# Sharing the products of a group between ScalarE and VectorE in a token-times-weights kernel

## The chip, the cores and the metric

The kernel runs on one core of a Trainium2 chip. The metric is the device time of one execution in microseconds (us). The core has a vector engine (VectorE, DVE in the profile), a scalar engine (ScalarE, ACT), a matrix engine (TensorE, PE), GpSimd (POOL) and a sync engine (SyncE, SP). ScalarE and SyncE issue transfers too; their queues are called ACTq and SPq, and 16 DMA engines carry out what both queues issue.

## What is computed

For each of 16 x 1024 tokens the row of 512 numbers is multiplied by each of the token's two weights, so every row of x gives two rows of the output. The expert indices are not used.

```python
batch, seq, hidden, n_experts, k = 16, 1024, 512, 8, 2
x_expanded = x[:, :, np.newaxis, :].repeat(k, axis=2)
weights = expert_weights[..., np.newaxis]
return (x_expanded * weights).astype(np.float32)
```

That reads 33.6 MB of x and writes 67.1 MB, all float32.

## The kernel before

The 16,384 tokens are cut into 8 groups of 2,048: 128 partitions with T = 16 tokens in each. A group lives in one slot of 64 KB per partition (16 tokens x 2 products x 512 numbers x 4 bytes), and there are three slots. The load of a group (`load`, L120, issued on ScalarE's queue, 4 MB) puts its x into the upper half of the slot; the products then fill the slot from below, in place. In units of 512 numbers, token t's x lies at position 16 + t and its products go to 2t and 2t + 1. So token t may be computed only when the tokens whose x lies at 2t and 2t + 1, tokens 2t - 16 and 2t - 15, have been read.

`ranges(16)` cuts the first 15 tokens into pieces that keep this rule: (0,8), (8,12), (12,14), (14,15). For each piece `products` issues one tensor_tensor on VectorE (L136), which broadcasts x over the two products and the weights over the 512 numbers: 8192, 4096, 2048 and 1024 numbers per partition. Token 15 is left to `last` (L151 to L157), two ACTIVATEs of 512 numbers on ScalarE (L153); the first of them overwrites token 14's x, the second token 15's own x.

The order of the work is written out by hand (manual schedule), so each engine executes its instructions in program order, and a tracker inserts the waits between engines where the tiles' regions meet. First the weights are loaded and spread over the partitions by TensorE transposes (L66 to L102), and the loads of groups 0, 1 and 2 are issued. Then, for each group i: the four products, the two ACTIVATEs, the store of the whole slot on SyncE's queue (L178, 8 MB), and, from group 1 on, the load of group i + 2, which goes into the slot of group i - 1 and so waits on ScalarE's queue until the store of group i - 1 has landed. In the first and the last group the store is in halves: the first 8 tokens right after the first product (L174), the rest at the end (L178).

Of the kernel before, what the change touches and what calls it, by code (L numbers as in the profile page):

```python
# [1 line left out]

# [4 lines left out]


@with_exitstack
def kernel(  # L10
    ctx: ExitStack,
    tc: tile.TileContext,
    x: bass.AP,
    expert_indices: bass.AP,
    expert_weights: bass.AP,
    out: bass.AP,
):
    nc = tc.nc

    batch, seq, hidden = x.shape  # L20
    k = expert_weights.shape[-1]
    P = nc.NUM_PARTITIONS
    ntok = batch * seq
    assert ntok % P == 0

    f32 = mybir.dt.float32
    row = k * hidden


    groups = [16] * 8  # L30
    assert sum(groups) * P == ntok
    TX = max(groups)

    xf = x.rearrange("b s h -> (b s) h")
    of = out.rearrange("b s k h -> (b s) (k h)")
    wf = expert_weights.rearrange("b s k -> (b s) k")

    w_pool = ctx.enter_context(tc.tile_pool(name="w_pool", bufs=1))
    slots = ctx.enter_context(tc.tile_pool(name="slots", bufs=3))
    raw_pool = ctx.enter_context(tc.tile_pool(name="raw_pool", bufs=1))  # L40
    psum = ctx.enter_context(
        tc.tile_pool(name="psum", bufs=2, space=bass.MemoryType.PSUM)
    )

    w_tile = w_pool.tile([P, sum(groups) * k], f32)

    def rows(flat, done, T):
        return flat[done * P : (done + T) * P, :].rearrange("(p a) n -> p (a n)", a=T)

    B = 8
    M = P // B
    ident = w_pool.tile([P, P], f32)
    nc.gpsimd.memset(ident, 0.0)  # L55
    nc.gpsimd.affine_select(  # L56
        out=ident,
        in_=ident,
        compare_op=mybir.AluOpType.not_equal,
        fill=1.0,  # L60
        base=0,
        pattern=[[-1, P]],
        channel_multiplier=1,
    )

    def weights_in(head, G, T):  # L66
        raw_tile = raw_pool.tile([G * M, B * T * k], f32, name=f"raw{T}_tile")
        nc.sync.dma_start(
            out=raw_tile,
            in_=wf[head * P : (head + G * T) * P, :].rearrange(  # L70
                "(q a) n -> q (a n)", a=B * T
            ),
        )
        return raw_tile

    def weights_spread(raw_tile, head, G, T):
        n = T * k
        col_tile = raw_pool.tile([n, G * P], f32, name=f"col{T}_tile")
        cols = col_tile.rearrange("c (q r) -> c q r", r=B)
        step = 4  # L80
        for r0 in range(0, B, step):
            up_tile = psum.tile([n, step, G * M], f32)
            for r in range(step):
                nc.tensor.transpose(  # L84
                    up_tile[:, r, :],
                    raw_tile[:, (r0 + r) * n : (r0 + r + 1) * n],
                    ident[: G * M, : G * M],
                )
            nc.vector.tensor_copy(  # L89
                out=cols[:, :, r0 : r0 + step],  # L90
                in_=up_tile.rearrange("c r q -> c q r"),
            )
        down_tile = psum.tile([P, G * n], f32)
        for g in range(G):
            nc.tensor.transpose(  # L95
                down_tile[:, g * n : (g + 1) * n],
                col_tile[:, g * P : (g + 1) * P],
                ident[:n, :n],
            )
        nc.vector.tensor_copy(  # L100
            out=w_tile[:, head * k : (head + G * T) * k], in_=down_tile
        )  # L102

    ctx.enter_context(tc.manual_schedule())

    starts = [sum(groups[:i]) for i in range(len(groups))]
    loaded = []

    def load(i):
        if i >= len(groups):
            return
        T = groups[i]
        slot_tile = slots.tile([P, TX * row], f32)
        loaded.append(slot_tile)
        src = rows(xf, starts[i], T)
        at = T * (row - hidden)
        nc.scalar.dma_start(out=slot_tile[:, at : at + T * hidden], in_=src)  # L120


    def ranges(T):
        lo, out = 0, []
        while lo < T - 1:
            hi = lo + 1
            while (hi + 1) * k <= T * (k - 1) + lo and hi < T - 1:
                hi += 1
            out.append((lo, hi))
            lo = hi  # L130
        return out

    def products(slot_tile, T, lo, hi, w_at):
        m = hi - lo
        at = T * (row - hidden) + lo * hidden
        nc.vector.tensor_tensor(  # L136
            out=slot_tile[:, lo * row : hi * row].rearrange(
                "p (t k h) -> p t k h", t=m, k=k
            ),
            in0=slot_tile[:, at : at + m * hidden]  # L140
            .rearrange("p (t h) -> p t h", t=m)
            .unsqueeze(2)
            .to_broadcast([P, m, k, hidden]),
            in1=w_tile[:, w_at + lo * k : w_at + hi * k]
            .rearrange("p (t k) -> p t k", t=m)
            .unsqueeze(3)
            .to_broadcast([P, m, k, hidden]),
            op=mybir.AluOpType.mult,
        )

    def last(slot_tile, T, w_at):  # L151
        for c in range(T * k - k, T * k):
            nc.scalar.mul(  # L153
                out=slot_tile[:, c * hidden : (c + 1) * hidden],
                in_=slot_tile[:, T * row - hidden : T * row],
                mul=w_tile[:, w_at + c : w_at + c + 1],
            )  # L157

    raw_tile = weights_in(0, 8, 16)
    load(0)  # L160
    load(1)
    load(2)
    weights_spread(raw_tile, 0, 8, 16)

    for i, T in enumerate(groups):
        slot_tile = loaded[i]
        outr = rows(of, starts[i], T)
        w_at = starts[i] * k
        done = 0
        for lo, hi in ranges(T):  # L170
            products(slot_tile, T, lo, hi, w_at)
            if i in (0, len(groups) - 1) and done == 0:
                done = hi
                nc.sync.dma_start(  # L174
                    out=outr[:, : done * row], in_=slot_tile[:, : done * row]
                )
        last(slot_tile, T, w_at)
        nc.sync.dma_start(  # L178
            out=outr[:, done * row :], in_=slot_tile[:, done * row : T * row]
        )  # L180
        if i:
            load(i + 2)

# [1 line left out]
_INS = ['x', 'expert_indices', 'expert_weights']  # L185
_OUTS = [((16, 1024, 2, 512), 'float32')]


# [23 lines left out]
```

## Time and profile before

| what | value |
|---|---|
| median of three runs (lowest to highest) | 248.65 us (239.22 to 249.16) |
| the profiled execution's own time | 239.3 us |
| its span, from the first to the last instruction | 237.5 us |
| moved between HBM and the core over the span | 100.80 MB, 424 GB/s |
| VectorE busy | 134.7 us (57%) |
| ScalarE busy | 12.8 us (5%) |
| TensorE busy | 2.9 us (1%) |
| a load, from issue to landing (median) | 32.6 us |
| a whole store, from issue to landing (median) | 35.9 us |

All views below come from one execution, taken by the hardware profiler. Rows of groups of instructions read: line, engine, operation, output <- inputs, shapes, count | busy time in us, mean duration of one in ns | idle time of the engine just before them and what ended most of it. Rows of the timeline read: start in us, length in us, engine, line, operation; in brackets the idle time before, with its releaser. Consecutive instructions of a kind are merged into one row, which then names the shape of the first. Rows of the table by stage read: from:to in us, its length, then the busy time of PE, PEld, DVE, ACT and POOL with the instructions begun or running, the granted clock of TensorE, the share of the DMA engines that was busy, and GB/s. Bytes are counted where a packet's record ends or begins, so single stages can read over 1.00.

### The profile page before, as it was taken

The page shows a single profiled execution, that of the slowest core. Times are in us where ns is not written, and L with a number is a line of the kernel's source. Part 1 is how long each engine was busy: PE and PEld are TensorE (multiplying, and loading weights), DVE is VectorE, ACT ScalarE, POOL GpSimd, SP SyncE. Part 2 cuts the span into 40 slices and gives each one's busy share as a digit, 9 for nine tenths or more (in the row PEclk, how much of TensorE's full clock was granted, in tenths as well). Part 3 has the DMA queues.
Part 4 walks back from the last instruction along what each step waited for, and adds up shares of the span by engine and source line. Part 5 has one row for each costly group of instructions (what it writes and reads, how often), then busy time and mean ns, then how long its engine had stood idle before and what let it go on. Part 6 is the DMA issues. An engine that isn't in the chain of part 4 may idle for free.

```text
span 237.5 us, 184 instructions
## 1 busy us (share of the span) xinstructions
PE 2.9 (1%) x16; PEld 1.9 (1%) x16; DVE 134.7 (57%) x35; ACT 12.8 (5%) x17; POOL 0.7 (0%) x6
## 2 busy tenths in 40 slices
PE   0400000000000000000000000000000000000000
PEld 0300000000000000000000000000000000000000
DVE  0289999999600089900998009970199602995000
ACT  0020020110200000020001100020000200002000
POOL 1000000000000000000000000000000000000000
DMA  7999999999899899899799898998998989989996
GB/s 284 444 441 441 353 441 441 436 447 441 375 419 530 353 441 530 353 441 530 337 458 430 370 524 353 441 530 353 441 530 348 447 386 453 486 353 441 441 441 265
DMA packets 2736, 100.80 MB, mean 424 GB/s; under 512 B 304, under 2 KB 432, under 8 KB 432
## 3 DMA queue, kind: packets, MB, share of 16 engines
q1 hardware_dynamic: 1584, 67.24, 65.5%
q10 hardware_dynamic: 1152, 33.55, 33.2%
HBM read 33.69 MB, written 67.11 MB: 424 GB/s over the span
## 4 chain that ended last, share of the span: by engine, by line
DMA 61%; DVE 28%; ACT 2%; issue 0%; DVEq 0%; ACTq 0%
DMA slot_tile<-in_x_dram 33%; DMA out_dram<-slot_tile 29%; DVE slot_tile L136 28%; ACT slot_tile L153 2%; DVEq L136 0%; ACTq L120 0%
## 5 line engine op out<-in xcount | busy, mean ns | idle before, releaser
L136 DVE TENSOR_TENSOR slot_tile<-slot_tile,w_tile 128x8192 f32<-128x8192 f32 (+3 forms) x32 | 132.9, 4158 | 71.6 <-DMA slot_tile<-in_x_dram 70.7
L153 ACT ACTIVATE slot_tile<-slot_tile,w_tile 128x512 f32<-128x512 f32 x16 | 11.5, 721 | 192.5 <-DVE slot_tile L136 192.3
L89 DVE COPY col_tile<-up_tile 32x512 f32<-32x512 f32 x2 | 1.4, 678 | 9.6 <-PE up_tile L84 9.6
L153 ACT ACT_TABLE_LOAD x1 | 1.3, 1283 | 13.2 <-DMA slot_tile<-in_x_dram 13.2
L84 PE MATMUL up_tile<-ident,raw_tile 128*32 128x128 f32 x8 | 1.9, 411 | 8.4 <-DMA raw_tile<-in_expert_weights_dram 8.4
L84 PEld LDWEIGHTS up_tile<-ident,raw_tile 128*32 128x32 f32 x8 | 1.0, 135 | 8.8 <-issue 8.4
L100 DVE COPY w_tile<-down_tile 128x256 f32<-128x256 f32 x1 | 0.4, 424 | 1.1 <-PE down_tile L95 1.1
L95 PE MATMUL down_tile<-ident,col_tile 32*128 32x32 f32 x8 | 1.1, 292 | 0.8 <-DVE col_tile L89 0.8
L95 PEld LDWEIGHTS down_tile<-ident,col_tile 32*128 32x128 f32 x8 | 0.9, 214 | 1.3 <-DVE col_tile L89 1.3
L56 POOL TENSOR_SCALAR_AFFINE_SELECT ident<-ident 128x128 f32<-128x128 f32 x1 | 0.3, 292 | 0.1
L55 POOL MEMSET ident<- 128x128 f32 x1 | 0.2, 204 | 0.3 <-POOLq L196 0.3
L196 POOL MEMSET const-bfloat16-1.0<- 128x1 bf16 x1 | 0.1, 101 | 0.0
L196 POOL MEMSET const-uint8-127<- 128x1 uint8 x1 | 0.1, 101 | 0.0
L196 POOL MEMSET const-float32-0.0<- 128x1 f32 x1 | 0.1, 98 | 0.2 <-issue 0.2
L196 POOL MEMSET const-float32-1.0<- 128x1 f32 x1 | 0.1, 98 | 0.0
## 6 DMA issues: line engine op xcount, KB each, us to landing
slot_tile<-in_x_dram ACTq DMA_DIRECT2D x8, 4096.0 KB, 32.6
out_dram<-slot_tile SPq DMA_DIRECT2D x4, 4096.0 KB, 19.5
raw_tile<-in_expert_weights_dram SPq DMA_DIRECT2D x1, 128.0 KB, 7.5
out_dram<-slot_tile SPq DMA_DIRECT2D x6, 35.9
```

What stands on the lines that cost most here:

```text
L55: nc.gpsimd.memset(ident, 0.0)
L56: nc.gpsimd.affine_select(out=ident, in_=ident, compare_op=mybir.AluOpType.not_equal, fill=1.0, base=0, pattern=[[-1, P]], channel_multipl ...
L84: nc.tensor.transpose(up_tile[:, r, :], raw_tile[:, (r0 + r) * n : (r0 + r + 1) * n], ident[: G * M, : G * M],)
L89: nc.vector.tensor_copy(out=cols[:, :, r0 : r0 + step], in_=up_tile.rearrange("c r q -> c q r"),)
L95: nc.tensor.transpose(down_tile[:, g * n : (g + 1) * n], col_tile[:, g * P : (g + 1) * P], ident[:n, :n],)
L100: nc.vector.tensor_copy(out=w_tile[:, head * k : (head + G * T) * k], in_=down_tile)
L136: nc.vector.tensor_tensor(out=slot_tile[:, lo * row : hi * row].rearrange("p (t k h) -> p t k h", t=m, k=k), in0=slot_tile[:, at : at + m ...
L153: nc.scalar.mul(out=slot_tile[:, c * hidden : (c + 1) * hidden], in_=slot_tile[:, T * row - hidden : T * row], mul=w_tile[:, w_at + c : w_ ...
L196: nc = _bacc.Bacc("TRN2", target_bir_lowering=False, num_devices=1)
```

## The change

`ranges` and `last` go. A new function `scaled` computes one token by two instructions, one for each weight: two ACTIVATEs on ScalarE or two tensor_scalars on VectorE. ScalarE now makes tokens 6 and 7 in the first half of a group and token 11 in the second; VectorE makes tokens 0 to 5, 8 to 10, 12 and 13, and 14 by tensor_tensors as before, and token 15 by two tensor_scalars at the end. The store of a half in the first and last group comes after the first 8 tokens, as before, and `load` stays as it is.

```diff
-    def ranges(T):
-        lo, out = 0, []
-        while lo < T - 1:
-            hi = lo + 1
-            while (hi + 1) * k <= T * (k - 1) + lo and hi < T - 1:
-                hi += 1
-            out.append((lo, hi))
-            lo = hi
-        return out
...
-    def last(slot_tile, T, w_at):
-        for c in range(T * k - k, T * k):
-            nc.scalar.mul(
-                out=slot_tile[:, c * hidden : (c + 1) * hidden],
-                in_=slot_tile[:, T * row - hidden : T * row],
-                mul=w_tile[:, w_at + c : w_at + c + 1],
-            )
+    def scaled(eng, slot_tile, T, t, w_at):
+        at = T * (row - hidden) + t * hidden
+        for c in range(t * k, t * k + k):
+            out = slot_tile[:, c * hidden : (c + 1) * hidden]
+            x_in = slot_tile[:, at : at + hidden]
+            w = w_tile[:, w_at + c : w_at + c + 1]
+            if eng is nc.scalar:
+                eng.mul(out=out, in_=x_in, mul=w)
+            else:
+                eng.tensor_scalar(
+                    out=out, in0=x_in, scalar1=w, scalar2=None, op0=mybir.AluOpType.mult
+                )
+
+    def first_half(slot_tile, T, w_at):
+        products(slot_tile, T, 0, 6, w_at)
+        scaled(nc.scalar, slot_tile, T, 6, w_at)
+        scaled(nc.scalar, slot_tile, T, 7, w_at)
+
+    def second_half(slot_tile, T, w_at):
+        scaled(nc.scalar, slot_tile, T, 11, w_at)
+        products(slot_tile, T, 8, 11, w_at)
+        products(slot_tile, T, 12, 14, w_at)
+        products(slot_tile, T, 14, 15, w_at)
+        scaled(nc.vector, slot_tile, T, 15, w_at)
...
-        for lo, hi in ranges(T):
-            products(slot_tile, T, lo, hi, w_at)
-            if i in (0, len(groups) - 1) and done == 0:
-                done = hi
-                nc.sync.dma_start(
-                    out=outr[:, : done * row], in_=slot_tile[:, : done * row]
-                )
-        last(slot_tile, T, w_at)
+        first_half(slot_tile, T, w_at)
+        if i in (0, len(groups) - 1):
+            done = T // 2
+            nc.sync.dma_start(
+                out=outr[:, : done * row], in_=slot_tile[:, : done * row]
+            )
+        second_half(slot_tile, T, w_at)
         nc.sync.dma_start(
             out=outr[:, done * row :], in_=slot_tile[:, done * row : T * row]
         )
```

## The prediction

> **What bounds the kernel now.** I first read the page's slices, queues and chain, to see which resource is full. The digits are tenths of a slice's time, the queue rows give packets, bytes and the share of the time of all 16 DMA engines.
>
> ```profile
> span 237.5 us, 184 instructions
> ...
> DVE  0289999999600089900998009970199602995000
> ...
> DMA  7999999999899899899799898998998989989996
> ...
> q1 hardware_dynamic: 1584, 67.24, 65.5%
> q10 hardware_dynamic: 1152, 33.55, 33.2%
> ...
> DMA 61%; DVE 28%; ACT 2%; issue 0%; DVEq 0%; ACTq 0%
> ```
>
> The stores' queue (q1) and the loads' queue (q10) together take 65.5 + 33.2 = 98.7% of the engines' time. So at most 1.3% of 237.5 us, 3.1 us, is left in which the transfers could be packed more tightly. VectorE shows empty slices from the middle on. The chain gives VectorE 28%, but a chain follows one releaser at each step; that the transfers behind that releaser were standing in a queue is not in it. So the next view is transfers by stage. Its last two columns are the busy share of the DMA engines and GB/s.
>
> ```profile
> 2.00:24.00 22.00, 2.92 (x16) 1.93 (x16) 12.54 (x5) 1.28 (x1) 0.00 (x0) 1.00 1.02 430
> 24.00:36.00 12.00, 0.00 (x0) 0.00 (x0) 11.93 (x4) 1.44 (x2) 0.00 (x0) 1.00 0.97 393
> 36.00:60.00 24.00, 0.00 (x0) 0.00 (x0) 23.83 (x7) 1.44 (x2) 0.00 (x0) 1.00 1.01 437
> 60.00:114.00 54.00, 0.00 (x0) 0.00 (x0) 20.60 (x7) 2.88 (x4) 0.00 (x0) 1.00 1.01 437
> 114.00:168.00 54.00, 0.00 (x0) 0.00 (x0) 32.51 (x8) 2.89 (x4) 0.00 (x0) 1.00 0.99 428
> 168.00:200.00 32.00, 0.00 (x0) 0.00 (x0) 16.64 (x4) 1.44 (x2) 0.00 (x0) 1.00 1.06 457
> 200.00:218.00 18.00, 0.00 (x0) 0.00 (x0) 16.64 (x4) 0.92 (x2) 0.00 (x0) 1.00 0.94 408
> 218.00:236.00 18.00, 0.00 (x0) 0.00 (x0) 0.00 (x0) 0.53 (x1) 0.00 (x0) 1.00 0.94 408
> ```
>
> The DMA share is 0.94 or more in every stage, whether VectorE is busy for 23.83 of 24 us (36 to 60) or for none of 18 (218 to 236). The rate has a plateau of 437 GB/s, and computing less would not raise it. The third view, the timeline, shows how much room stands between the arithmetic and the transfers.
>
> ```profile
> 101.05 1.48 ACT L153 ACTIVATE slot_tile<-slot_tile,w_tile 128x512 f32<-128x512 f32 x2 [36.31 <-DVE slot_tile L136]
> 109.53 0.33 ACTq L120 DMA_DIRECT2D slot_tile<-in_x_dram  x1
> 113.24 16.74 DVE L136 TENSOR_TENSOR slot_tile<-slot_tile,w_tile 128x8192 f32<-128x8192 f32 x4 [12.22 <-DMA slot_tile<-in_x_dram]
> 130.01 1.47 ACT L153 ACTIVATE slot_tile<-slot_tile,w_tile 128x512 f32<-128x512 f32 x2 [27.48 <-DVE slot_tile L136]
> 131.51 29.37 SPq L178 DMA_DIRECT2D out_dram<-slot_tile  x2
> 138.49 0.33 ACTq L120 DMA_DIRECT2D slot_tile<-in_x_dram  x1
> 142.27 16.74 DVE L136 TENSOR_TENSOR slot_tile<-slot_tile,w_tile 128x8192 f32<-128x8192 f32 x4 [12.29 <-DMA slot_tile<-in_x_dram]
> ```
>
> A load (L120) goes into the slot that a store has just left, so its issue marks that store's landing. Group 3 is computed at 101.05 + 1.48 = 102.53 and its store can be queued, but the store of group 2 lands only at 109.53: the new store stands 7.0 us in line. Group 4 repeats it: queued at 131.51, the store ahead landing at 138.49, again 7.0 us. Meanwhile VectorE waits 12.3 us per group for a load.
>
> **The change part by part.** The durations of one group are these:
>
> ```profile
> L136 DVE TENSOR_TENSOR slot_tile<-slot_tile,w_tile 128x8192 f32<-128x8192 f32 x8 | 69.5, 8691 | 70.7 <-DMA slot_tile<-in_x_dram 70.7
> L136 DVE TENSOR_TENSOR slot_tile<-slot_tile,w_tile 128x4096 f32<-128x4096 f32 x8 | 35.4, 4425 | 0.3
> L136 DVE TENSOR_TENSOR slot_tile<-slot_tile,w_tile 128x2048 f32<-128x2048 f32 x8 | 18.3, 2292 | 0.3
> L153 ACT ACTIVATE slot_tile<-slot_tile,w_tile 128x512 f32<-128x512 f32 x16 | 11.5, 721 | 192.5 <-DVE slot_tile L136 192.3
> L136 DVE TENSOR_TENSOR slot_tile<-slot_tile,w_tile 128x1024 f32<-128x1024 f32 x8 | 9.8, 1225 | 0.3
> ...
> L89 DVE COPY col_tile<-up_tile 32x512 f32<-32x512 f32 x2 | 1.4, 678 | 9.6 <-PE up_tile L84 9.6
> ```
>
> *Before*, one after the other: 8.69 + 4.43 + 2.29 + 1.23 + 2 x 0.72 = 18.1 us; with the gaps it is 131.51 - 113.24 = 18.27 us from the first product to the store's issue. One token of VectorE's products costs (8691 - 4425) / 4 = 1066 ns, with 4425 - 4 x 1066 = 161 ns for each instruction.
>
> *VectorE's products after*: six tokens 161 + 6 x 1066 = 6.56 us, three tokens 3.36, two 2.29, one 1.23: 13.44 us.
>
> *The two tensor_scalars of token 15*: no row shows this form. The nearest is the 512-element copy, 0.68 us, though it reads PSUM and covers 32 partitions; the line of the products gives 161 + 533 = 0.69. The other end is the fixed 0.16 us alone. I take 0.69, 1.39 for both; the low end is 0.32. The Trainium skill, "VectorE: DVE Perf Modes", the perf-mode tier table, has fp32 tensor_scalar from SBUF at twice the rate of tensor_tensor; worked out from its 1227 ns for 2048 elements and its 0.96 GHz, an estimate for 512 is 0.43 us, and a group would be 0.5 us shorter than my sum. No run here shows it yet.
>
> *Sum of a group after*: 13.44 + 1.39 + 0.1 of gaps = 14.9 us (13.9 to 15.0 between the ends), 3.3 us less than 18.27. The first half is ready after 6.56 instead of 8.69 us, 2.1 us earlier.
>
> *ScalarE*: six ACTIVATEs instead of two, 6 x 0.72 = 4.3 us, beside the products. Tokens 6 and 7 end after 2.9 us, under VectorE's 6.56; token 11 after 4.4 us, when VectorE reaches tokens 12 and 13, which overwrite token 11's input, after 6.56 + 3.36 = 9.9 us. The cover is 5.5 us. Without it the four first ACTIVATEs would add 2.9 us and token 11 another 1.4. In group 0 the 1.28 us that ScalarE is busy between 2 and 24 (its table load) come first, inside the same cover.
>
> *The wait that moves*: ScalarE's queue also issues the loads, and the load of group i+2 waits there until the store of group i-1 has landed. Before, that stood ahead of two late ACTIVATEs; now six early ones of group i+1 are behind it. In the steady part the wait is over at 109.53 and the next slot's data come at 113.24, 138.49 and 142.27 likewise: 3.7 us to spare. Group 2 is the exception:
>
> ```profile
> 13.21 50.03 DVE L136 TENSOR_TENSOR slot_tile<-slot_tile,w_tile 128x8192 f32<-128x8192 f32 x12 [0.66 <-DMA slot_tile<-in_x_dram]
> ...
> 52.81 0.33 ACTq L120 DMA_DIRECT2D slot_tile<-in_x_dram  x1
> 63.27 1.48 ACT L153 ACTIVATE slot_tile<-slot_tile,w_tile 128x512 f32<-128x512 f32 x2 [15.17 <-DVE slot_tile L136]
> ```
>
> The first three groups run without a break on VectorE, from 13.21 on. Two groups of 14.9 us later it starts group 2 at about 43 and reaches token 12 at 53, while ScalarE is free at 52.8 and done with token 11 at 57.3: VectorE waits some 4.3 us. The group ends at 57.3 + 2.29 + 1.23 + 1.39 = 62.2, still before today's 63.27 + 1.48 = 64.75. Cost nothing.
>
> *The transfers*: number, size and queues of all loads and stores stay; the first and last group are still stored in halves of 8 tokens. In the steady part a store is queued 3.3 us earlier and stands 10.3 instead of 7.0 us in line: 0 us. The start: the first store leaves 2.1 us earlier into engines that are already 1.02 busy: 0 us, with the low stage of 24 to 36 as the room. The end:
>
> ```profile
> 200.28 16.74 DVE L136 TENSOR_TENSOR slot_tile<-slot_tile,w_tile 128x8192 f32<-128x8192 f32 x4 [12.27 <-DMA slot_tile<-in_x_dram]
> 209.00 0.33 SPq L174 DMA_DIRECT2D out_dram<-slot_tile  x1
> 217.05 1.48 ACT L153 ACTIVATE slot_tile<-slot_tile,w_tile 128x512 f32<-128x512 f32 x2 [27.53 <-DVE slot_tile L136]
> 218.55 0.33 SPq L178 DMA_DIRECT2D out_dram<-slot_tile  x1
> ```
>
> The two stages after 200 move 36 us x 408 GB/s = 14.7 MB. The last group is 8.4 of it, so 6.3 MB of group 6's store are still due at 200, good until 200 + 6.3 / 0.437 = 214.4. The first half of the last store (4.2 MB, queued at 209.0) lasts until 224, the second is queued at 218.55: each comes 5 us before it is needed. They will come at 206.9 and 215.2. Gain 0, at most the shortfall of the rate: (437 - 408) / 437 x 36 = 2.4 us, if it came from single DMA engines that ran dry early. I take 0.3 us of it, near zero because the shares stay at 0.94 through both stages, also where the whole store is already queued.
>
> *Sum*: the profiled execution took 239.3 us (span 237.5 and 1.8 around it). 239.3 - 0.3 = **239.0 us**. The median of the three runs shown is 248.65, 9.35 above this execution, the lowest 239.22 and the highest 249.16; nothing in the profile at hand shows what the longer ones spent the time on.
>
> **The rivals.** *The gaps close (faster).* If earlier stores brought every stage below the plateau up to it: 24 to 36 gives (437 - 393) / 437 x 12 = 1.2 us, 114 to 168 (437 - 428) / 437 x 54 = 1.1, the end 2.4; 4.7 in all, 234.6 us, the bound of 2%. For it speaks that these are the stages with arithmetic at the start and the end. Against it: 218 to 236 has no arithmetic left, all is queued, and the rate is the same 408; the stage of 168 to 200 is above the plateau, so part is a matter of where packets are counted. The executions of 249 may also hold a wait that ends with the change; then the same kernel would read 4% faster against their median, at about 239.
>
> *The transfers themselves run slower (slower).* The stores start earlier, so loads and stores may meet in another order. If the mixed stages from 36 to 200 ran at the 408 of the last ones instead of 437, they would take 164 x (437 / 408 - 1) = 11.7 us more: 251 us. It passes 2% once the mean over them falls below 164 / 168.8 x 437 = 425. That the same instructions also took 249.16 shows that such a loss exists; against it, the mixed stages keep to 428 to 457 for 164 us and the change leaves their bytes and queues alone. The Trainium skill has a harsher form of it: "DMA: Bandwidth & Descriptors", "Where 436 GB/s comes from", says that between HBM and SBUF the HBM side binds at about 358 GB/s for a core; by that 100.8 MB would take 282 us, an estimate, and this trace contradicts it with 437 over 78 us.
>
> *ScalarE is held up behind the load's wait (within 2%).* If the store of group i-1 landed d after the data of group i+1, VectorE would stop at token 12 once d is over 5.5 us, and the queue of stores would only be short when the 10.3 us in line are used up too, at d = 15.8 us. Today d is -3.7. At d = 10 a group takes 4.5 us longer, the store still stands 5.8 us in line, and the time stays 239, or 241 if half of the 4.5 reached the end once.
>
> **How the numbers follow.** No change 0.68; ScalarE held up, still within 2%, 0.08; gaps closed or the long executions cured 0.12; slower transfers 0.12. A difference of 2% is about what a measurement of this kernel tells from no change. So faster 0.12, same 0.76, slower 0.12. The likeliest case alone lies in 236.2 (3.1 us of idle share gone) to 241. The range goes from 235.0, by the rival that closes the gaps, to 249.5, which takes in the longest execution shown and most of the slower transfers.
>
> **What would show it.** The products on VectorE fall from 133.0 us (the four rows above) to 8 x 14.83 = 119 us, and ScalarE's ACTIVATEs rise from 11.5 to 48 x 0.72 = 35 us. From first product to store it is 14 to 15 us per group. The stores stand some 10 us in line in the steady part, VectorE waits for loads 15 to 16 us per group instead of 12.3, and the two queues still take 98% or more. Wrong would be: a mean rate under 425 between 36 and 200, VectorE waiting on ScalarE in the steady groups, or a span under 234.

## The result and the profile after

| | changed kernel | kernel before, on the same chip |
|---|---|---|
| six executions, us | 250.23, 249.19, 248.54, 251.14, 249.73, 251.86 | 248.65, 249.16, 239.22, 249.99, 239.39, 247.45 |
| median, us | 249.98 | 248.05 |

The ratio of the measurement is 1.0452, 95% interval 1.0358 to 1.0546: slower. It counts the two executions of the kernel before near 239 us and leaves out its four others; over all six the medians differ by 0.8%. The forecast was 239.0 us and no change, with a range up to 249.5. So the time fell just outside the range, and the question is what makes 239 of 249, and whether the change has a part in it.

The page of the changed kernel, the rows that answer to those of before:

```profile
span 248.4 us, 238 instructions
...
DVE  0289998957000059700796003990039900697000
...
DMA  7999999999989999989999989899989999989961
...
q1 hardware_dynamic: 1584, 67.24, 63.8%
q10 hardware_dynamic: 1152, 33.55, 32.6%
...
DMA 68%; DVE 23%; issue 1%; DVEq 0%; ACTq 0%; SPq 0%
```

The bytes are the same. The two queues take 96.4% instead of 98.7%, and the last digits of the DMA row fall off over two slices instead of one. The groups of instructions by shape:

```profile
L124 DVE TENSOR_TENSOR slot_tile<-slot_tile,w_tile 128x6144 f32<-128x6144 f32 x8 | 52.5, 6557 | 95.5 <-DMA slot_tile<-in_x_dram 95.5
L149 ACT ACTIVATE slot_tile<-slot_tile,w_tile 128x512 f32<-128x512 f32 x48 | 30.3, 709 | 172.4 <-DMA slot_tile<-in_x_dram 146.1 <-DVE slot_tile L124 26.3
L124 DVE TENSOR_TENSOR slot_tile<-slot_tile,w_tile 128x3072 f32<-128x3072 f32 x8 | 26.9, 3358 | 0.3
L124 DVE TENSOR_TENSOR slot_tile<-slot_tile,w_tile 128x2048 f32<-128x2048 f32 x8 | 18.3, 2292 | 5.3 <-ACT slot_tile L149 4.1 <-DVE slot_tile L124 0.5
L124 DVE TENSOR_TENSOR slot_tile<-slot_tile,w_tile 128x1024 f32<-128x1024 f32 x8 | 9.8, 1224 | 0.3
L151 DVE TENSOR_SCALAR slot_tile<-slot_tile,w_tile 128x512 f32<-128x512 f32 x16 | 7.8, 486 | 0.6
```

VectorE has less to do than before (115.3 us in these rows instead of 133.0) and waits 95.5 instead of 70.7 us for loads. Arithmetic isn't what got longer. The timeline of two groups in the steady part:

```profile
119.63 13.61 DVE L124 TENSOR_TENSOR slot_tile<-slot_tile,w_tile 128x6144 f32<-128x6144 f32 x4 [15.36 <-DMA slot_tile<-in_x_dram]
...
133.27 1.01 DVE L151 TENSOR_SCALAR slot_tile<-slot_tile,w_tile 128x512 f32<-128x512 f32 x2
134.35 33.50 SPq L185 DMA_DIRECT2D out_dram<-slot_tile  x2
145.52 0.33 ACTq L119 DMA_DIRECT2D slot_tile<-in_x_dram  x1
...
152.80 13.60 DVE L124 TENSOR_TENSOR slot_tile<-slot_tile,w_tile 128x6144 f32<-128x6144 f32 x4 [18.52 <-DMA slot_tile<-in_x_dram]
```

A group takes 134.35 - 119.63 = 14.7 us, and its store then stands 145.52 - 134.35 = 11.2 us in line. From one group's data to the next it is 152.80 - 119.63 = 33.2 us, where the kernel before needed 29.0 for the same bytes. The table by stage says at what rate:

```profile
36.00:60.00 24.00, 0.00 (x0) 0.00 (x0) 19.14 (x9) 3.78 (x6) 0.00 (x0) 1.00 1.02 437
60.00:114.00 54.00, 0.00 (x0) 0.00 (x0) 16.08 (x9) 3.78 (x6) 0.00 (x0) 1.00 1.02 425
114.00:168.00 54.00, 0.00 (x0) 0.00 (x0) 28.81 (x12) 7.57 (x12) 0.00 (x0) 1.00 0.98 416
168.00:200.00 32.00, 0.00 (x0) 0.00 (x0) 14.40 (x6) 3.78 (x6) 0.00 (x0) 1.00 1.02 422
200.00:218.00 18.00, 0.00 (x0) 0.00 (x0) 4.41 (x1) 3.78 (x6) 0.00 (x0) 1.00 1.00 433
218.00:236.00 18.00, 0.00 (x0) 0.00 (x0) 9.99 (x6) 0.00 (x0) 0.00 (x0) 1.00 0.93 399
236.00:248.40 12.40, 0.00 (x0) 0.00 (x0) 0.00 (x0) 0.00 (x0) 0.00 (x0) 1.00 0.40 172
```

Up to 60 us the rate is that of before. From 36 to 200 the mean is 423 instead of 438 GB/s: 164 x (438 / 423 - 1) = 5.8 us. The busy share stays at 0.98 to 1.02 all the same, so the engines were not idle; some packets held them longer. The rest of the 10.9 us is in the tail: after 236 us still 2.1 MB move at a share of 0.40. By the landings of the last store thirteen engines are done by 242.0 us, and three only at 246.9 to 247.3.

How the engines take their packets is seen in the GB/s row of the queues' view, here over the 12 us from 150 to 162 in 40 steps. Bytes are counted at one point of each packet, so 16 engines that start their packets together, in step, make a comb. First the kernel before, then the changed one:

```profile
GB/s 0 0 0 765 983 0 0 1311 2185 0 0 0 0 0 0 655 1092 0 0 1092 2403 0 0 0 0 0 0 546 1092 109 0 1092 2185 218 0 0 0 0 0 437
```

```profile
GB/s 218 109 874 1092 437 218 218 218 0 218 437 437 328 328 1092 874 765 218 109 0 218 109 765 437 328 328 874 1092 655 218 109 109 0 109 546 874 218 328 765 1311
```

In the kernel before all engines take a load packet (the low tooth, 32 KB each), then all a store packet (the high tooth, 64 KB), 3.6 us a turn. In the changed kernel some are at a load while others are at a store. Worked out from the packet and landing records of the two traces:

```
                                              before      after
64 KB packets of stores, mean / longest, ns   2418/2440   2478/3827
packets over 30 ns longer than the usual one,
  after 50 us, and by how much together       0           231, 78.3 us
first to last of the 16 engines to land,
  worst transfer, us                          0.4         14.5
last store: first / last engine, us           236.0/236.4 240.9/247.3
```

The 78.3 us are 4.9 us for each of the 16 engines, close to the 5.8 us above. A load counts as landed only with the last engine's share: one in the changed kernel landed on the first engine at 116.01 us and on the last at 119.61, and its products began at 119.63. So one late engine holds all.

### The profile page after: what moved, and what is told of

It is laid out like the page before. It is cut to its first block, busy times and chain, and to the rows that moved or that the text cites. A ratio compares the mean times of both kernels' runs of the same rounds, so it can differ in the third digit from the quotient of the medians.

```text
span 248.4 us, 238 instructions
## 1 busy us (share of the span) xinstructions
PE 2.9 (1%) x16; PEld 1.9 (1%) x16; DVE 116.9 (47%) x51; ACT 31.6 (13%) x49; POOL 0.7 (0%) x6
## 3 DMA queue, kind: packets, MB, share of 16 engines
q10 hardware_dynamic: 1152, 33.55, 32.6%
## 4 chain that ended last, share of the span: by engine, by line
DMA 68%; DVE 23%; issue 1%; DVEq 0%; ACTq 0%; SPq 0%
DMA slot_tile<-in_x_dram 35%; DMA out_dram<-slot_tile 33%; DVE slot_tile L124 22%; DVE slot_tile L151 2%; DVEq L124 0%; ACTq L119 0%; SPq L185 0%
## 5 line engine op out<-in xcount | busy, mean ns | idle before, releaser
L124 DVE TENSOR_TENSOR slot_tile<-slot_tile,w_tile 128x6144 f32<-128x6144 f32 (+3 forms) x32 | 107.5, 3358 | 101.3 <-DMA slot_tile<-in_x_dram 95.5
L149 ACT ACTIVATE slot_tile<-slot_tile,w_tile 128x512 f32<-128x512 f32 x48 | 30.3, 709 | 172.4 <-DMA slot_tile<-in_x_dram 146.1
L151 DVE TENSOR_SCALAR slot_tile<-slot_tile,w_tile 128x512 f32<-128x512 f32 x16 | 7.8, 486 | 0.6
```

Source lines behind the costliest of these rows:

```text
L124: nc.vector.tensor_tensor(out=slot_tile[:, lo * row : hi * row].rearrange("p (t k h) -> p t k h", t=m, k=k), in0=slot_tile[:, at : at + m ...
L149: eng.mul(out=out, in_=x_in, mul=w)
L151: eng.tensor_scalar(out=out, in0=x_in, scalar1=w, scalar2=None, op0=mybir.AluOpType.mult)
```

## The experiments

Three theories. A (step): both kernels can run with the 16 engines in step or out of step, and out of step the alternation of packets costs about 10 us; the change has no part in it. B: the change itself puts the engines out of step, or costs otherwise. C: slow memory from outside, whatever the kernel.

### The changed kernel again, unaltered (three more times)

No edit.

> The changed kernel once more, unaltered. Theory A (step): both kernels have two ways to run, 239 us with the 16 DMA engines in step and 247 to 252 us with them out of step; which one comes is settled when the load of group 3 (issued near 52.8 us) first meets the store of group 1, and the change has no part in it. Then the changed kernel shows some executions near 239 too, about as often as the kernel before (2 of 6). Theory B (the change): the earlier stores, or ScalarE's work beside VectorE's, put the engines out of step; then all its executions stay at 248 to 252 us while the kernel before keeps some at 239. Theory C (from outside): slow memory for some executions, whatever the kernel; both kernels mixed, as in A.

Six executions: 249.03, 243.08, 246.93, 250.46, 239.9, 248.22; the kernel before beside it 242.68 to 251.48, median 248.67 of 11.

> The changed kernel unaltered, a third time, for the share of its executions near 240 us. So far 2 of 12 lay under 244 us, and 5 of 28 of the kernel before. Theory A: one or two of six under 244 us, the others at 246 to 252 us, the median within 2% of the kernel before beside it. Theory B: none under 244 us and a median over 2% above the kernel before.

239.84, 239.98, 239.93, 240.09, 239.98, 245.47, while the kernel before on that chip had 10 of 11 above 246 (median 247.97). The profile of this run, of the unaltered changed kernel:

```profile
span 238.1 us, 238 instructions
...
q1 hardware_dynamic: 1584, 67.24, 65.3%
q10 hardware_dynamic: 1152, 33.55, 33.1%
```

The teeth are there in the same 12 us:

```profile
GB/s 0 0 0 655 983 109 0 1311 1966 218 0 0 0 0 0 655 983 109 0 1311 1966 218 0 0 0 0 0 655 983 109 0 1311 1966 218 0 0 0 0 0 655
```

98.4% and a comb: the changed kernel in step takes 238.1 us of span, 0.6 more than the kernel before in step. Theory B in its strict form falls.

The profile of the set before it (again_after, span 247.3 us) shows that a long execution needs no more than one late engine: fifteen engines landed the last store at 237.3 to 238.3 us, about as early as in step, and the sixteenth at 246.1.

> The kernel before, unaltered, loaded as a kernel of its own, beside the same kernel as the common baseline. If what decides between 239 and 249 us is drawn anew in each execution, its share under 244 us is that of the baseline (6 of 39 so far, so 0 to 2 of six). If it is settled when a program is loaded, its executions lie on one side (five or six of six), whichever the baseline's do.

246.14, 246.81, 247.16, 249.08, 248.3, 249.65: none under 244, with the common baseline at 1 of 11 (239.59). Its own profile is out of step too, and has three engines late by up to 9.9 us:

```profile
GB/s 328 0 109 2185 655 218 218 0 0 437 0 983 437 0 0 1966 874 109 0 218 0 218 0 1420 437 0 0 1748 1092 0 109 0 218 0 218 874 983 0 0 1748
```

> The changed kernel unaltered, a fourth time. So far 0, 2 and 5 of six lay under 244 us in three loads of it. Drawn in each execution: about 2 of six (7 of 18). Settled at loading: five or six of six on one side. Theory B: none under 244 us.

249.29, 249.61, 251.4, 243.26, 250.08, 249.34.

Over all executions of the unaltered kernels, 7 of 56 executions of the kernel before lie under 244 us and 8 of 24 of the changed one; the medians are 247.63 and 248.79, ratio 1.005 (0.983 to 1.008, by drawing anew from the two lists). The means are 247.36 and 246.52, so the order of the two kernels turns with the way of averaging. Neither guess on when it is settled holds cleanly: the changed kernel's four sets went 0, 2, 5 and 1 of six, more bunched than a draw for each execution would make likely, but three of the four were mixed. What settles it stays open.

### The first meeting of a load and a store, moved

In the profile of before, the load of group 3 started on all 16 engines at one packet boundary, 56.82 to 57.21 us. In the changed kernel's, 11 engines took one more store packet there (56.85 to 57.20) and 5 the load (57.15 to 57.31), and the packets were stretched from there on. So a load that comes in the middle of a packet should find all engines at the same boundary.

```diff
+        if i == 3:
+            nc.scalar.mul(out=slot_tile[:, at : at + hidden],
+                          in_=loaded[1][:, :hidden], mul=w_tile[:, :1])
         nc.scalar.dma_start(out=slot_tile[:, at : at + T * hidden], in_=src)
```

> The kernel before, with one ACTIVATE of 512 numbers in the freed slot ahead of the load of group 3, so that this load is issued about 0.9 us later after the store's landing (53.7 instead of 52.8 us). In the profile of before the load's first packets started at 56.82 to 57.21 us, 4.0 us after the issue, just at a packet boundary of all engines; in the changed kernel some engines missed that boundary. Theory A: 0.9 us later all 16 engines are in the middle of a 2.4 us store packet, all take the load at the next boundary, and every execution is near 239 us (237 to 241). Theory B: as the kernel before, some at 239 and some at 248 to 250. Theory C: the same mixture as the kernel before, beside it on the same chip.

239.83 to 251.73, median 249.5, two of six under 244. The load was issued at 53.92 and all 16 engines took it in one round, at 59.28 to 59.97 us, yet from 70 us on packets were stretched. A miss: to meet in step is not enough to stay in step.

> The changed kernel with the same one ACTIVATE ahead of the load of group 3. Theory A: every execution near 239 us (237 to 241), as the kernel before with the same delay, so the change is worth nothing either way. Theory B: 248 to 252 us, as the changed kernel without it. Theory C: a mixture of both.

239.71, 252.15, 239.83, 239.83, 239.91, 251.84: four of six near 239.8. With one such set for each kernel, this doesn't show that the delay did it.

The kernel before with the same delay and, besides, a small load that should put half of the engines out of step (only this second edit is shown):

```diff
+        if i == 1:
+            nc.scalar.dma_start(out=slot_tile[:8, at : at + T * hidden], in_=src[:8, :])
```

> The kernel before with the delayed load of group 3, and with one more small load: partitions 0 to 7 of group 1 are loaded once more ahead of its load (8 packets of 32 KB, 0.26 MB, on 8 of the 16 engines), which puts half of the engines one packet of 1.2 us behind the others. Theory A: the halves take the load of group 3 at different times, stay out of step, packets of stores are stretched over 2.42 us, and the time is 246 to 252 us. Theories B and C: 0.26 MB more at 437 GB/s is 0.6 us, so the same as the kernel with the delay alone, within 2 us.

248.58 to 261.5, median 258.84. Inconclusive: the load of group 1 waited for the small one to land, and the table by stage has a hole that was not meant.

```profile
12.00:18.00 6.00, 2.01 (x13) 1.26 (x11) 4.50 (x4) 0.00 (x0) 0.00 (x0) 1.00 0.29 44
```

After the hole all engines started together, and stayed together until 144 us (landings 0.5 us apart at most).

### The start

The changed kernel with the same delay and, besides, the first loads held until the weights have landed (only this second edit is shown):

```diff
+    warm = raw_pool.tile([P, 1], f32)
+    nc.scalar.mul(out=warm, in_=raw_tile[:, :1], mul=1.0)
     load(0)
```

> The changed kernel with the delayed load of group 3 and with the first loads of x held until the weights have landed, so that the first packets of x don't meet those of the weights. In the profiles so far the 16 engines' landings of the first load lay 0.30 and 0.53 us apart in the two executions at 239 us and 0.61 to 0.77 us in those at 247 to 250 us. Theory A: the start is later by 2 to 6 us, the spread of the first landing is under 0.4 us, and most executions are 4 to 10 us faster than 249, at 240 to 245 us, without any near 250. If the spread comes from elsewhere: the mixture of 240 to 252 us, plus 2 to 6 us. Theory C: the same mixture, plus 2 to 6 us.

253.96 to 255.24, median 254.44. The loads start 2.1 us later (2.86 instead of 0.74), and the first landing is 0.43 us wide, yet all six executions are long. In earlier profiles first landings up to 0.53 us wide went with 239 us, so a narrow first landing isn't enough, and that explanation falls.

### One queue

Both kernels with all loads on the stores' queue, so that no engine alternates between two queues:

```diff
-        nc.scalar.dma_start(out=slot_tile[:, at : at + T * hidden], in_=src)
+        nc.sync.dma_start(out=slot_tile[:, at : at + T * hidden], in_=src)
```

> The kernel before with its loads issued on SyncE's queue, behind the stores in program order, so that each of the 16 DMA engines has one row of packets and never chooses between a load and a store. Theory A (step: an engine whose loads and stores alternate out of step with the other engines loses time): there is no alternation any more, no packet of a store is stretched over 2.42 us, the landings of the 16 engines stay within 1 us of each other, and all executions lie at 237 to 241 us, median 8 to 10 us under the kernel before beside it. Theory C (slow memory from outside, whatever the kernel): the same mixture as the kernel before, most executions at 246 to 252 us. If SyncE's waits on a store's landing hold up the next store instead, the time is over 245 us in all executions with a DMA share under 0.95.

> The changed kernel with its loads on SyncE's queue. Theory A: 237 to 241 us in all executions, within 1% of the kernel before in the same form, since the transfers cover the arithmetic of both (about 6 us to spare in the kernel before, 10 us here). Theory B (the change itself costs 4%): about 249 us, 10 us over the kernel before in the same form. Theory C: a mixture.

Kernel before with one queue: 240.99 to 242.85, median 242.18. Changed kernel: 240.25 to 243.11, median 241.94, 0.1% less. The kernel before as it is, on the same chip: 242.11 to 251.38, median 247.46. No execution is near 249 any more, which theory C can't give. The store packets of the first are all of 2418 ns. The medians are 1 us over the 241 I had set as the upper end, and 5.3 us under the kernel before where 8 to 10 were expected; in the profile of the first, one engine lags by up to 3.7 us without stretched store packets, and the page shows the same bytes at a share of 97.5%:

```profile
span 241.1 us, 182 instructions
...
q1 hardware_dynamic: 2736, 100.80, 97.5%
```

### Packets of one length

A slot of 64 KB per partition goes out in 64 KB packets, x comes in with 32 KB. The changed kernel with all stores in halves:

```diff
-        if i in (0, len(groups) - 1):
+        if True:
             done = T // 2
```

> The changed kernel with the store of every group in two halves of 8 tokens, as in the first and the last group, so that packets of loads and of stores are both 32 KB. Theory A: an engine that misses a turn then has a load against the others' store of the same length; whether it is stretched as with 64 KB packets is not known: if out of step is what costs, the mixture stays (240 to 252 us); if unequal lengths are what costs, all executions lie at 237 to 241 us. Theory C: the same mixture as the kernel before.

239.98 to 241.33, median 240.08; the kernel before beside it 247.46. Unequal lengths, then, rather than step alone. Is it the halves' earlier start? Here both halves are queued at the group's end:

```diff
         second_half(slot_tile, T, w_at)
+        if done == 0:
+            done = T // 2
+            nc.sync.dma_start(out=outr[:, : done * row], in_=slot_tile[:, : done * row])
```

> The changed kernel with the store of every group in two halves, both queued only when the whole group is computed (first and last group as before): packets of 32 KB as in the version with halves, but no earlier store. Theory A1: packets of one length for loads and stores are what removes the loss; then 239 to 242 us in all executions. Rival: the earlier first half of each store is what removes it; then the mixture of 240 to 252 us, median over 246.

239.96 to 240.93, median 240.34: the packets, not the earlier start. Is it that 64 KB is long? Halves of 32 KB for stores and of 16 KB for loads:

```diff
-        nc.scalar.dma_start(out=slot_tile[:, at : at + T * hidden], in_=src)
+        half = T * hidden // 2
+        for c in (0, half):
+            nc.scalar.dma_start(out=slot_tile[:, at + c : at + c + half], in_=src[:, c : c + half])
```

> The changed kernel with stores in halves (32 KB packets) and loads in two halves too (16 KB packets): the ratio of the lengths is 2 to 1 as in the unaltered kernel, at half the size. Theory A1 (unequal lengths cost): the mixture returns, most executions at 244 to 252 us. Theory A2 (only the long 64 KB packets cost): 239 to 242 us in all executions.

240.81 to 252.55, median 245.91, five of six over 244. The mixture is back with packets half as long, so it isn't the length of 64 KB; what the two mixtures have in common is the ratio of two to one. That two loads for each group bring it back by themselves was not tested. Its page:

```profile
span 244.2 us, 278 instructions
...
q1 hardware_dynamic: 2448, 67.24, 64.3%
q10 hardware_dynamic: 2304, 33.56, 32.6%
```

### The change by itself, where the alternation is harmless

The kernel before with `if done == 0:` for its condition, so that its stores go in halves as well.

> The kernel before with the store of every group in two halves of 8 tokens, the first right after the first product. The changed kernel in this form ran at 240.0 to 241.3 us in all of six executions. If the change is worth nothing either way (theory A), this one lies at 239 to 242 us in all executions as well, within 1% of the changed kernel in the same form. If the change costs by itself (theory B), it is under 235 us; if the shorter arithmetic of the change is what made the halves work, it shows the mixture of 240 to 252 us.

239.43 to 240.19, median 239.65, on a chip where the kernel as it is had 247.97. On another chip, side by side with the changed kernel in the same form:

> The kernel before with all stores in halves, beside the changed kernel in the same form on one chip: the direct measure of the change where the alternation of packets costs nothing. Theory A: 239 to 241 us, and the two medians within 0.5% (1.2 us). Theory B: the changed kernel in this form over 2% above.

> The changed kernel with all stores in halves, on the same chip as the kernel before in that form. Theory A: 239 to 241 us, within 0.5% of it. Theory B: over 2% above it.

Kernel before in halves 239.37 to 240.43, median 239.72; changed kernel in halves 240.76 to 242.04, median 241.46: ratio of the means 1.007 (1.004 to 1.009, worked out from the two sets of six). In the queues' view, the same 12 us, the first is a comb, the second is not:

```profile
GB/s 1420 328 0 0 1311 437 0 0 1201 546 0 0 1201 546 0 0 983 765 0 0 983 765 0 0 983 765 0 0 874 874 0 0 874 874 0 0 874 874 0 0
```

```profile
GB/s 983 328 109 328 983 328 109 328 983 218 218 328 983 218 218 328 874 328 218 328 874 328 218 328 874 328 218 328 874 328 218 328 874 328 218 328 765 437 218 328
```

The expected 0.5% was missed; on two other chips the medians of the same two forms were 239.65 (before) and 240.08 (changed). So with packets of one length an execution can be out of step and still take only 241 to 242 us. The half-version of the kernel before is the best one measured: 3.2% under the kernel as it is on that chip (247.72), without the change.

## Why the prediction was right or wrong

*The arithmetic* held. A group takes 14.7 us (forecast 14.9), VectorE's products 115.3 us (119), ScalarE's 48 x 0.709 = 34 us (35). The tensor_scalar took 486 ns where I had put 690 from the nearest row. The estimate from the Trainium skill, "VectorE: DVE Perf Modes", the perf-mode tier table, was 0.43 us, so its doubled rate agrees with the trace but for 0.06 us. VectorE's wait for ScalarE in group 2, forecast at 4.3 us, was 4.1, and it occurred nowhere else, as said: in the steady part ScalarE was free 152.80 - 145.52 = 7.3 us before the data.

*The store in line*: forecast 10.3 us, found 11.2. That the shorter group gives back nothing is right: VectorE waits for loads in the steady stage of every profile. How long was misjudged: 15 to 16 us per group were forecast, and in step (again_after2) it waited 14.2 to 14.5. The forecast added the whole 3.3 us of the group to 12.3, but token 15 went from ScalarE to VectorE, so VectorE's own work fell by only 16.7 - 14.6 = 2.1 us.

*What failed* is the first term of the sum, 239.3 us, with the plateau of 437 GB/s that the step "The transfers" rests on. The forecast took the time and the rate of one execution for properties of the kernel as long as both queues are filled, and left the two runs at 249 as unexplained. In the changed kernel's profile the queues were filled (share 0.98 to 1.02 in the steady stages), and from 60 to 200 us the rate was 416 to 425. The rate also depends on whether the 16 engines alternate in step, and the execution profiled was one of the few that did. Of the sum, 239.0 for the changed kernel in step was near (239.8 to 240.1 in five of six executions of one set); as the usual time of either kernel it was wrong by 9 to 10 us. The usual time was in the forecast's own table, as the median of the runs shown. The 0 us that "The transfers" gave to the change itself stands.

*The rival "The transfers themselves run slower"* came near in size: 251 us forecast, 249.98 measured, its bound of 425 GB/s from 36 to 200 us passed with 423. That is partly luck. It put 11.7 us into these stages, by a rate of 408; they cost 5.8, and the other 5.1 came in the tail, where three engines were late, which it didn't have. Its cause was not shown there, and the change is not it: the unaltered kernel before does the same in 49 of 56 executions. The Trainium skill's harsher figure, about 358 GB/s for a core between HBM and SBUF ("DMA: Bandwidth & Descriptors", "Where 436 GB/s comes from"), is contradicted out of step as well, by 416. Another section of that page of the Trainium skill fits better: "Queues, rings and completion order" says that each DMA engine goes round its queue rows packet by packet. The traces agree, one load packet and one store packet in turn; what it costs when engines do so out of step with unequal packets, the runs here show.

*"Gaps close (faster)"* had an aside that the executions of 249 might hold a wait which ends with the change. The change ends nothing of the kind: 16 of 24 executions of the unaltered changed kernel are long too.

*No change* is what the change itself is worth, within 1%: -0.1% on one queue, +0.7% in halves, +0.5% by the medians of the unaltered lists (-0.3% by their means). The last pair is loose, 0.983 to 1.008, and whether the change alters how often an execution is long (16 of 24 against 49 of 56) is open. Shown is that the loss goes when loads and stores are on one queue (12 executions, none over 243.11 us) or have packets of one length (30 executions, none over 242.04). Not shown are why a packet is stretched when other engines are at the other kind, and what throws an execution out of step. Equal packets change one thing more: a load then lands in a median of 22.9 us (kernel before in halves) instead of 32.6. Whether this or the equal length itself removes the loss was not separated; with one queue it goes although a load takes 35.7 us. The last 0.7% in halves goes along with an execution out of step (landings up to 4.6 us apart against 0.4), and isn't proven to be the change's.

## What to carry to other kernels

A DMA share of 98% in one profile says that transfers bind; it doesn't say that their rate is fixed, and when several runs of the same kernel lie 4% apart, the spread is the first thing to explain. Where loads and stores run on two queues at once, try packets of the same length (here 32 KB per partition each, by storing in halves); in this kernel that was worth 3%, while 3.5 us less arithmetic in each group was worth nothing. And look at when each engine lands its share, not only at the mean: between 36 and 200 us the mean share in the stages of the long executions was still 0.98 to 1.03.

## What the runs showed of the hardware

The 16 DMA engines, each alternating between two queues, stayed in step in some executions and drifted apart in others of the same program: the changed kernel's landings were at most 1.0 us apart in one execution (again_after2) and up to 15.0 in another (again_after), the kernel before's 0.4 and 9.9 (before, again_before). A 64 KB store packet took 2418 ns in step, with few exceptions, and up to 3827 in the first profile of the changed kernel. One late engine is enough: in again_after (span 247.3 us) fifteen engines landed within 0.6 us of each other up to 210 us, and the sixteenth was up to 15.0 us late. The six ACTIVATEs of a group took 3.79 us together, 0.63 each, where one alone takes 0.72.
